# Two-layer streaming encoder step: branch scalars, load order, last tile and five small operations changed at once

## The chip, the cores and the metric

The kernel runs on one core of one Trainium2 chip. The metric is the device time of one execution in microseconds (us). A core has five engines with an instruction queue each, which run side by side and wait for each other by semaphores: PE (TensorE, matmuls; PEld is its weight load), DVE (VectorE), ACT (ScalarE), POOL (GpSimd), and SP, which here only issues DMAs. Each engine takes its instructions strictly in the order in which the program lists them.

## The reference

The reference is one inference step of an encoder with two layers, for a prompt of 512 frames and a sample request of 32 frames with 1024 frames of cache. The 544 frames are carried together, frames along the free dimension (`T` = 544) and 8 tiles of 128 model columns on the partitions. One layer is

```
h = RMSNorm(x);  z = h @ w_in                       (all mixers and gates in one projection)
A = latent attention (q from a rank-256 latent, keys from a rank-128 latent, rotary key)
B = stick-breaking attention (reverse cumulative sums of log(1 - sigmoid))
C = (softmax(Q1 K1) - lambda * softmax(Q2 K2)) V, per-head norm, times (1 - lambda_init)
    lambda = exp(sum(lv0*lv1)) - exp(sum(lv2*lv3)) + lambda_init   (one scalar per layer)
x += w_out(sigmoid(gA)*(A @ wA) + sigmoid(gB)*(B @ wB) + sigmoid(gC)*(C @ wC))
x += w_down(silu(conv3(a)) * u),   [a, u] = RMSNorm(x) @ w_up
```

and besides y the new rows of all caches and the last two rows of the convolution are returned. All matmuls are done in float32r with each operand split in a high and a low part (three products), so each weight tile is first rounded on ACT (high part) and subtracted on DVE (low part).

## The kernel before

**Order of the work.** The program is not written in the order in which it runs. `Sched` (L114) keeps a clock for each engine and a list of fibers, Python generators with a time `ready`. `Sched.run` steps the fiber with the smallest `ready` first; each helper (`act`, `tt`, `ptt`, `dscale`, `mm`, ...) emits one instruction and adds an estimated price to its engine's clock. So the estimated times decide in which order instructions stand in each engine's queue, and after that the queues are fixed. A fiber that is spawned with `low=True` is put behind PE's clock by `LOW` (L138). Constants at L95 to L106 set this planner: `WIDTH` is how many attention fibers may be open at once, `LO` is the place in the list of branch projections from which the last eight attention outputs are loaded back.

**Weights.** `Stream.loader` (L214) is a fiber that issues one DMA on SP for each weight tile (128x1024 f32, 512 KB), in the order of `plan()`, into 4 buffers `ws`. `Stream.splitter` (L228) splits each tile in halves of 512 columns into 4 buffers `wx`: high part on ACT (L340), low part on DVE (L347).

**Start of the program** (`run`, L2143). SP issues the gains of layer 0 (L2162), then the four vectors of lambda (L2186), the first weight tile, and the eight input tiles `x_in` (L2250). Each input tile is scaled and split on ACT and DVE (`norm_tile`, L528); its squares are summed over the tiles, and `norm_rows` (L555) makes the reciprocal root: a split of the sum, four matmuls with a constant matrix, logarithm and exponential on ACT.

**Per layer.** The loop at L2178 loads ACT's table, loads the vectors of lambda into a `tf` buffer and works out lambda and four gain columns by some ten tiny operations on DVE and one exponential on ACT (L2189 to L2204); these are emitted at once, outside of the planner, and for both layers into the same small tiles. Then `attention` runs: projections of the units (`qkv_tasks`, 48 matmuls of 128x272 for each tile of 128 columns), gate projections between them (`gate_tasks`, 24 a layer, 48 matmuls each), and the chains of the three mixers: units 0 to 3 stick-breaking (`sb`), 4 to 7 differential (`df`), 8 to 11 latent (`ml`). `GATES` (L42) tells how many gate projections follow the projections of each of the 12 units, the last digit being those that run with low priority beside the last unit. Then follow the branch projections `br_tasks`, `out_tasks`, the up projections (a Strassen form for most), and the down projections `down_tasks` (L2115) in two halves of 11 tiles each.

**Two-operand operations on GpSimd.** `ptt` (L350) emits a tensor_tensor on POOL. It is used in five places: the low part of the differential keys (`to_stack`, L662), the running sums of the stick-breaking sample (L943, seven of 128x64 a unit) and prompt (`sb_sum`, L1098), and the rotary product of the latent queries (L1521, 64x544). POOL also rounds high parts (`pscale`, L367), scales softmax rows, and issues some DMAs.

**End.** The last eight down projections add into x by halves of 272 columns on DVE; `fin` (L2238) stores the whole tile as y (layer 1) or as xs (layer 0). With `both=True` a `gemm` (L445) does the two halves of a tile side by side in two PSUM banks; with `both=False` all steps of the first half come before those of the second. After the planner has run dry, the convolution rows are stored (L2248).

Of the kernel before, what the change touches and what calls it, by code (L numbers as in the profile page):

```python
# [17 lines left out]
L = 2  # L18
# [23 lines left out]
GATES = "403111221315"  # L42
# [58 lines left out]
WIDTH = 12  # L101
LOW = 100.0
LO = 2
# [96 lines left out]
class Stream:  # L200
# [5 lines left out]
    def __init__(self, K, ap, pool):  # L206
        self.K, self.nc, self.s, self.ap, self.pool = K, K.nc, K.s, ap, pool
        self.plan = plan()
        self.early = [key for key, _ in self.plan[:2]]
        self.raw, self.parts = {}, {}  # L210
        self.s.spawn(self.loader(), daemon=True)
        self.s.spawn(self.splitter(), daemon=True)

    def loader(self):  # L214
        s, o = self.s, 0
        for key, n in self.plan:
# [94 lines left out]
class Kern:  # L311
# [216 lines left out]
    def norm_tile(self, m, x, gcol, l, R, late=0, tag="h"):  # L528
# [23 lines left out]
        if m == 7:  # L552
            self.s.spawn(self.norm_rows(R), daemon=True)
# [99 lines left out]
    def to_stack(self, dst, name, z, scale=1.0):  # L653
# [248 lines left out]
    def sb_sample(self, d, U):  # L902
# [38 lines left out]
        for kt in range(6, -1, -1):  # L941
            o, n = col(kt), col(kt + 1)
            self.ptt(R[:, o:o + 64], R[:, n:n + 64], t[:, n:n + 64], ALU.add)  # L943
# [150 lines left out]
    def sb_sum(self, U, h, j, t, sp):  # L1094

        if j < 3:
            yield from self.s.need(U, ("t", h, j + 1))
            self.ptt(t[:, 128:], t[:, 128:], U["t", h, j + 1][0], ALU.add)  # L1098
# [400 lines left out]
    def ml_prep(self, l, u, M, d):  # L1499

        def q_task(h):
# [13 lines left out]
            def post(box):  # L1515
# [5 lines left out]
                self.ptt(z[r], z[r], M["tq"][0][r], ALU.mult)  # L1521
# [593 lines left out]
    def down_tasks(self, l, hf, acts, X, fin):  # L2115
        def mk(m):
# [10 lines left out]
            def post(box):  # L2127
                x = X[m][0]
                for h in range(2):
                    g, c = yield from self.half(box, h)  # L2130
                    self.tt(x[:, c], g, x[:, c], ALU.add)
                    self.unbank(box, h)
                    yield
                if hf == 1:
# [4 lines left out]
                                     chunk, lambda k: self.s.need(acts, 11 * hf + k), free, True)  # L2139
# [3 lines left out]
    def run(self):  # L2143
        tc, nc, a, s = self.tc, self.nc, self.a, self.s
        with tc.tile_pool(name="P", bufs=1) as P, tc.tile_pool(name="ps", bufs=1, space=PSUM) as ps, \
# [5 lines left out]
            self.eps = P.tile([128, 1], F32, tag="eps", name="eps")  # L2151
            nc.vector.memset(self.eps, EPS)
            self.lamv = P.tile([128, 1], F32, tag="lamv", name="lamv")
            self.nlam = P.tile([128, 1], F32, tag="nlam", name="nlam")
            lw = P.tile([128, 8], F32, tag="lw", name="lw")
# [6 lines left out]
            nc.sync.dma_start(out=self.gpl[0], in_=a["gains"][0])  # L2162
            R = {}

# [13 lines left out]
            for l in range(L):  # L2178
                nc.scalar.preload_act_table_set("natural_log_exp_and_others")
                self.gp = self.gpl[l]  # L2180
                if l == 0:
                    s.spawn(consts(), 9000.0)
                    self.ws = Stream(self, a["wts"], P)
                lam_init = 0.8 - 0.6 * math.exp(-0.3 * l)
                lv = self.t(P, [128, T], "tf")
                nc.sync.dma_start(out=lv[:, :256], in_=a["lam"][l])  # L2186
                l4 = lv[:, :256].rearrange("p (a b c) -> p a b c", a=2, b=2)
                l2 = lv[:, 256:384].rearrange("p (a c) -> p a c", a=2)
                nc.vector.tensor_tensor(out=l2, in0=l4[:, :, 0], in1=l4[:, :, 1], op=ALU.mult)  # L2189
                nc.vector.tensor_reduce(out=lw[:, 0:2], in_=l2, op=ALU.add, axis=AX.X)  # L2190
                nc.scalar.activation(out=lw[:, 2:4], in_=lw[:, 0:2], func=AF.Exp)
                nc.vector.tensor_tensor(out=lw[:, 4:5], in0=lw[:, 3:4], in1=lw[:, 2:3], op=ALU.subtract)
                nc.vector.tensor_scalar(out=self.nlam, in0=lw[:, 4:5], scalar1=-lam_init, scalar2=None, op0=ALU.add)
                nc.vector.memset(self.lamv[:32], 1.0)
                nc.vector.tensor_copy(out=self.lamv[32:64], in_=self.nlam[32:64])
                sg = self.gain(G_SUB)
                nc.vector.tensor_scalar(out=sg, in0=sg, scalar1=1.0 - lam_init, scalar2=None, op0=ALU.mult)
                dq = self.gain(G_DQ)
                nc.vector.tensor_scalar(out=dq, in0=dq, scalar1=0.125, scalar2=None, op0=ALU.mult)
                mq = self.gain(G_QE, 2)  # L2200
# [309 lines left out]
```

## Time and profile before

| what | us |
|---|---|
| median of 3 runs (2080.33 to 2081.0) | 2080.8 |
| the profiled execution, its own time | 2081.47 |
| its span in the profile, first to last instruction | 2079.6 |
| PE busy | 2024.5 (97%) |
| DVE busy | 1619.2 (78%) |
| ACT busy | 1308.3 (63%) |
| POOL busy | 501.9 (24%) |
| mean granted TensorE clock | 0.997 |

The span is what the views of the trace cover; the execution's own time is 1.87 us longer. A busy share is an average over stages: layer 0 lies in about 0 to 1044 us of the span, layer 1 behind it, and in each the attention takes the first half. In a row of the timeline the first number is the start, the second the time, `xN` how many instructions were merged, and the bracket how long the engine sat idle before and what ended that. PEclk is the granted clock as a part of the full 2.4 GHz; 0.50 is 1.2 GHz.

### The profile page before, as it was taken

How to read it: one execution, taken by the hardware profiler on the slowest of the kernel's cores; microseconds unless marked ns; L12 is line 12 of the kernel's file. 1: busy time of each engine (PE TensorE's matmuls, PEld its weight loads, DVE VectorE, ACT ScalarE, POOL GpSimd, SP SyncE). 2: the span in 40 equal slices, each digit the busy share in tenths (PEclk: the TensorE clock that was granted, in tenths of full speed). 3: DMA queues.
4: the chain of work that ended last, by engine and by line, in shares of the span. 5: the costliest groups of instructions: out<-in, count | busy, mean ns of one | idle time of the engine just before them, and what ended most of it. 6: DMA issues, size and time to landing. Idle time of an engine off the chain costs nothing.

```text
span 2079.6 us, 41484 instructions
## 1 busy us (share of the span) xinstructions
PE 2024.5 (97%) x15638; PEld 1974.1 (95%) x15638; DVE 1619.2 (78%) x3435; ACT 1308.3 (63%) x2905; POOL 501.9 (24%) x810
## 2 busy tenths in 40 slices
PE   7999999999999999999989999999899999999999
PEld 7999999888999999999989999998899999999999
DVE  7888888888685996598567878988886869955973
ACT  6887676877554564366368777668775545644651
POOL 1333332334200221032023443313341002210310
PEclk9999999999999999999999999999999999999999
DMA  6333342321663222332433334343216622223332
GB/s 205 104 104 124 120 157 93 129 73 48 212 199 107 80 95 83 110 102 82 133 119 98 109 124 132 122 133 102 83 39 223 203 93 92 94 80 102 102 90 87
DMA packets 86216, 238.42 MB, mean 115 GB/s; under 512 B 10304, under 2 KB 11200, under 8 KB 86016
## 3 DMA queue, kind: packets, MB, share of 16 engines
q1 hardware_dynamic: 82240, 223.51, 33.7%
q0 software_dynamic: 3776, 12.26, 1.7%
q8 instruction: 123, 2.02, 0.4%
q14 instruction: 77, 0.63, 0.1%
HBM read 201.52 MB, written 34.21 MB: 113 GB/s over the span
## 4 chain that ended last, share of the span: by engine, by line
PE 75%; DVE 14%; ACT 5%; issue 4%; POOL 1%; DMA 1%; SPq 0%; POOLq 0%; ACTq 0%; DVEq 0%
PE z L410 40%; PE g L410 25%; PE pv L410 8%; DVE wx L347 2%; PE z L416 2%; DVE tf L347 1%; ACT p L340 1%; DVE w L347 1%; ACT wx L340 1%; ACT w L340 1%; DVE tr L347 1%; DVE kk L347 1%; ACT tf L340 1%; DVE nm L372 1%; DVE sgl L355 1%
## 5 line engine op out<-in xcount | busy, mean ns | idle before, releaser
L410 PE MATMUL g<-h,wx 128*128 128x272 f32 x5208 | 757.2, 292 | 9.1 <-ACT wx L340 9.0
L410 PEld LDWEIGHTS g<-h,wx 128*128 128x128 f32 x5208 | 695.6, 189 | 17.5 <-ACT wx L340 9.0
L410 PE MATMUL z<-act,wx 128*128 128x272 f32 x4632 | 586.7, 288 | 5.6 <-DVE wx L347 5.6
L410 PEld LDWEIGHTS z<-act,wx 128*128 128x128 f32 x4632 | 581.5, 189 | 6.7 <-DVE wx L347 6.7
L340 ACT ACTIVATE wx<-ws 128x512 fp32r<-128x512 f32 (+2 forms) x554 | 307.0, 555 | 383.9 <-PE z L410 257.1
L347 DVE TENSOR_TENSOR wx<-ws,wx 128x512 fp32r<-128x512 f32 (+2 forms) x554 | 343.7, 621 | 208.7 <-ACT wx L340 205.2
L410 PE MATMUL z<-h,wx 128*128 128x272 f32 x1368 | 179.6, 290 | 0.0
L410 PEld LDWEIGHTS z<-h,wx 128*128 128x128 f32 x1368 | 175.5, 191 | 0.0
L340 ACT ACTIVATE w<-z 128x512 fp32r<-128x512 f32 (+9 forms) x212 | 90.9, 440 | 52.4 <-PE pv L410 27.7
L347 DVE TENSOR_TENSOR tf<-g,rstd 128x272 f32<-128x272 f32 x184 | 79.8, 434 | 31.9 <-PE g L410 25.8
L2061 POOL COPY conv<-ap 128x2 f32<-128x2 f32 x34 | 20.7, 610 | 316.9 <-DVE ap L347 316.9
L1924 POOL COPY conv<-ap 128x2 f32<-128x2 f32 x10 | 19.5, 1953 | 299.8 <-DVE ap L347 299.8
L410 PE MATMUL pv<-w,vst 128*128 128x512 f32 (+3 forms) x352 | 85.5, 325 | 4.9 <-DVE w L347 4.3
L2048 POOL COPY ap<-gp 128x2 f32<-128x2 f32 x34 | 63.5, 1866 | 81.9 <-ACT wx L340 60.0
L340 ACT ACTIVATE wy<-ws 128x512 fp32r<-128x512 f32 x68 | 42.9, 630 | 60.1 <-PE z L410 34.9
L368 POOL TENSOR_SCALAR tr<-tf 128x544 fp32r<-128x544 f32 (+2 forms) x66 | 49.1, 744 | 128.2 <-ACT tf L340 89.2
L355 DVE SCALAR_TENSOR_TENSOR cc<-ap,gp,cc 128x546 f32<-128x546 f32 x88 | 69.2, 786 | 4.0 <-ACT cc L340 3.8
L340 ACT ACTIVATE p<-p 128x512 f32<-128x512 f32 (+4 forms) x160 | 70.6, 465 | 0.9
L340 ACT ACTIVATE wx<-sgl 128x512 fp32r<-128x512 f32 x102 | 63.4, 627 | 11.1 <-PE z L410 7.1
L347 DVE TENSOR_TENSOR wx<-sgl,wx 128x512 fp32r<-128x512 f32 x102 | 67.8, 686 | 2.3 <-ACT wx L340 2.2
L368 POOL TENSOR_SCALAR kk<-kk 64x1024 fp32r<-64x1024 f32 x32 | 40.7, 1272 | 118.3 <-DVE kk L347 101.0
L347 DVE TENSOR_TENSOR w<-z,w 128x512 fp32r<-128x512 f32 (+5 forms) x124 | 55.8, 465 | 15.3 <-ACT w L340 14.6
(274 smaller groups left out, 3673.0 us busy)
## 6 DMA issues: line engine op xcount, KB each, us to landing
ws<-wts SPq DMA_DIRECT2D x246, 512.0 KB, 3.6
ws<-wts SPq DMA_DIRECT2D x56, 256.0 KB, 3.0
ws<-wts SPq DMA_DIRECT2D x36, 384.0 KB, 3.0
sgl<-sig SPq DMA_DIRECT2D x46, 272.0 KB, 3.2
ws<-wts SPq DMA_DIRECT2D x32, 320.0 KB, 3.0
sig<-tf SPq DMA_DIRECT2D x36, 272.0 KB, 2.1
tf<-od POOLq DMA_DIRECT2D x24, 272.0 KB, 4.7
od<-oa SPq DMA_DIRECT2D x16, 272.0 KB, 2.3
```

Source lines behind the costliest of these rows:

```text
L340: self.nc.scalar.activation(out=out, in_=in_, func=func, **kw)
L347: self.nc.vector.tensor_tensor(out=out, in0=in0, in1=in1, op=op)
L355: self.nc.vector.scalar_tensor_tensor(out=out, in0=in0, scalar=scalar, in1=in1, op0=op0, op1=op1)
L368: self.nc.gpsimd.tensor_scalar(out=out, in0=in_, scalar1=s1, scalar2=1.0, op0=ALU.mult, op1=ALU.mult)
L372: self.nc.vector.tensor_reduce(out=out, in_=in_, op=op, axis=AX.X, negate=negate)
L410: self.nc.tensor.matmul(out=out, lhsT=lhsT, rhs=rhs, start=start, stop=stop, skip_group_check=not chk)
L416: self.nc.tensor.transpose(out, in_, self.ident[:p, :p])
L1924: nc.gpsimd.tensor_copy(out=cv[:, 0:2], in_=ap[:, 546:548])
L2048: nc.gpsimd.tensor_copy(out=ap[:, 0:2], in_=self.gain(G_ST + 2 * i, 2))
L2061: nc.gpsimd.tensor_copy(out=cv[:, 0:2], in_=ap[:, 546:548])
```

## The change

- The scalars of both layers (lambda and the scaled gains) are made by a fiber `lams`, spawned at the planner's 40 us in layer 0, into columns of one tile; nothing of this is left in the loop over the layers. The exponential and the small DVE operations go through the planner's helpers.
- The first weight tile is loaded in two halves by DMAs issued on ACT's queue, as are the gains of layer 0; the loader starts with the second tile, at the planner's 0.1 us, so that SP issues the eight input tiles first. The planner's estimates of when the input tiles land are changed (4.7 us + 0.8 us a tile in place of 3.0 + 1.1).
- `norm_rows` of the first norm of a layer is spawned 1 us later in the planner's time.
- All five `ptt` become `tt`, on DVE.
- `GATES`: one gate projection goes from behind unit 7 to behind unit 4. `WIDTH` 12 to 11, `LOW` 100 to 50, `LO` 2 to 3.
- In the last layer y is stored by halves as each is added, and the last of the eight tiles is done with `both=False`. The convolution rows are stored before the last down projection, in both layers.

```diff
-GATES = "403111221315"
+GATES = "403121211315"
-WIDTH = 12
-LOW = 100.0
-LO = 2
+WIDTH = 11
+LOW = 50.0
+LO = 3
@@ class Stream, __init__
+        s, t = K.s, K.t(pool, [128, 1024], "ws")
+        s.tok["ws"].pop()
+        for c in (0, 512):
+            self.nc.scalar.dma_start(out=t[:, c:c + 512],
+                                     in_=ap[:128 * 1024].rearrange("(p c) -> p c", p=128)[:, c:c + 512])
+        self.raw[self.plan[0][0]] = (t, 4500.0)
+        self.s.spawn(self.loader(), 100.0, daemon=True)
@@ loader
-        for key, n in self.plan:
+        for key, n in self.plan[1:]:
@@ norm_tile
-            self.s.spawn(self.norm_rows(R), daemon=True)
+            self.s.spawn(self.norm_rows(R), self.s.cur.ready + (1000.0 if tag == "h" else 0.0), daemon=True)
@@ to_stack; the same in sb_sample, sb_sum and ml_prep
-                self.ptt(out, x, f(hi), ALU.subtract)
+                self.tt(out, x, f(hi), ALU.subtract)
@@ down_tasks
+                    if y is not None:
+                        self.store(y[m][:, c], x[:, c])
-                                     chunk, lambda k: self.s.need(acts, 11 * hf + k), free, True)
+                                     chunk, lambda k: self.s.need(acts, 11 * hf + k), free, y is None or m < 7)
@@ run
-            nc.sync.dma_start(out=self.gpl[0], in_=a["gains"][0])
+            nc.scalar.dma_start(out=self.gpl[0], in_=a["gains"][0])
+            self.ws = Stream(self, a["wts"], P)
+            def lams():
+                for l in range(L):
+                    lv = yield from self.tf()
+                    nc.sync.dma_start(out=lv[:, :256], in_=a["lam"][l])
+                    s.cur.ready += 5000.0
+                    yield
...
+                    self.tt(l2, l4[:, :, 0], l4[:, :, 1], ALU.mult)
+                    yield
+                    nlam, lamv = lw[:, 1 + l:2 + l], lw[:, 3 + l:4 + l]
+                    self.red(lw[:, 8:10], l2, ALU.add)
+                    s.give("tf")
+                    yield
+                    self.act(lw[:, 10:12], lw[:, 8:10], AF.Exp)
+                    yield
...
             for l in range(L):
                 nc.scalar.preload_act_table_set("natural_log_exp_and_others")
                 self.gp = self.gpl[l]
+                self.nlam, self.lamv = lw[:, 1 + l:2 + l], lw[:, 3 + l:4 + l]
                 if l == 0:
                     s.spawn(consts(), 9000.0)
-                    self.ws = Stream(self, a["wts"], P)
-                lv = self.t(P, [128, T], "tf")
-                nc.sync.dma_start(out=lv[:, :256], in_=a["lam"][l])
...
-                nc.scalar.activation(out=lw[:, 2:4], in_=lw[:, 0:2], func=AF.Exp)
...
+                    s.spawn(lams(), 40000.0)
@@ end of the layer
-                    lst += self.down_tasks(l, 1, acts, X, fin)
+                    dn = self.down_tasks(l, 1, acts, X, fin, a["y"] if l == L - 1 else None)
+                    lst += dn[:-1] + [convs, dn[-1]]
...
-                    self.store(a["convo"][l], self.conv)
@@ x_in
-        self.s.cur.ready += 3000.0 + 1100.0 * m
+        self.s.cur.ready += 4700.0 + 800.0 * m
```

## Rows read from the trace of the kernel before

**Rows 1.** The page: busy time of the engines, and the chain by engine.
```profile
PE 2024.5 (97%) x15638; PEld 1974.1 (95%) x15638; DVE 1619.2 (78%) x3435; ACT 1308.3 (63%) x2905; POOL 501.9 (24%) x810
...
PE 75%; DVE 14%; ACT 5%; issue 4%; POOL 1%; DMA 1%; SPq 0%; POOLq 0%; ACTq 0%; DVEq 0%
```

**Rows 2.** Windows: length, busy us by engine (instructions), PEclk, DMA share, GB/s.
```profile
0.00:20.00 20.00, 10.92 (x63) 10.60 (x64) 12.58 (x28) 12.73 (x21) 0.66 (x6) 1.00 0.88 297
...
40.00:360.00 320.00, 315.39 (x2369) 301.42 (x2369) 269.44 (x634) 239.78 (x579) 112.13 (x210) 1.00 0.36 119
360.00:520.00 160.00, 150.34 (x1127) 141.44 (x1126) 133.70 (x289) 122.14 (x307) 59.87 (x80) 1.00 0.26 84
...
1080.00:1400.00 320.00, 317.20 (x2381) 303.38 (x2380) 265.33 (x631) 235.98 (x571) 113.31 (x207) 1.00 0.36 117
1400.00:1560.00 160.00, 149.46 (x1106) 140.31 (x1104) 131.86 (x288) 119.08 (x306) 60.29 (x81) 0.99 0.24 78
```

**Rows 3.** Timeline of the first 20 us.
```profile
1.26 0.42 SPq L2186 DMA_DIRECT2D tf<-lam  x1
...
2.19 1.85 SPq L2253 DMA_DIRECT2D tf<-x  x4
...
6.98 1.41 ACT L340 ACTIVATE h<-tf,gp 128x544 fp32r<-128x544 f32 x2 [2.46 <-DMA tf<-x]
...
8.29 0.61 ACT L340 ACTIVATE wx<-ws 128x512 fp32r<-128x512 f32 x1
...
8.96 9.45 PE L410 MATMUL g<-h,wx 128*128 128x272 f32 x48 [8.96 <-ACT wx L340]
...
18.24 6.89 PE L410 MATMUL z<-h,wx 128*128 128x272 f32 x54
```

**Rows 4.** Timeline of the boundary between the layers.
```profile
1044.13 0.38 SPq L2186 DMA_DIRECT2D tf<-lam  x1
...
1047.37 0.29 DVE L2189 TENSOR_TENSOR tf<-tf 128x128 f32<-128x128 f32 x1 [3.28 <-DMA tf<-lam]
...
1049.34 0.39 PE L410 MATMUL pv<-tr,cr 128*128 128x272 f32 x1 [2.95 <-ACT tr L340]
...
1050.85 1.05 PE L410 MATMUL pv<-tr,cr 128*128 128x272 f32 x3 [1.12 <-DVE tr L347]
...
1051.70 9.10 PE L410 MATMUL z<-h,wx 128*128 128x272 f32 x54
```

**Rows 5.** Window of 2 us behind the boundary's gap, same columns as rows 2.
```profile
1052.00:1054.00 2.00, 2.00 (x11) 2.00 (x11) 0.79 (x2) 1.08 (x2) 0.00 (x0) 0.50 0.75 242
```

**Rows 6.** Timeline of the last DMA issues.
```profile
2076.49 0.33 SPq L442 DMA_DIRECT2D y<-x  x1
2076.91 0.38 SPq L442 DMA_DIRECT2D convo<-conv  x1
```

**Rows 7.** Window over the whole span, instructions of L351 alone.
```profile
0.00:2079.60 2079.60, 100.34 (x128) 1.00 0.36 115
```

**Rows 8.** Groups of DVE by form: 0 to 30, 40 to 520, 1400 to 1560 us.
```profile
L347 DVE TENSOR_TENSOR wx<-ws,wx 128x512 fp32r<-128x512 f32 x7 | 4.8, 687 | 3.8 <-ACT wx L340 3.8
...
L347 DVE TENSOR_TENSOR an<-z,an 128x64 f32<-128x64 f32 x4 | 0.8, 210 | 0.0
...
L347 DVE TENSOR_TENSOR wx<-ws,wx 128x512 fp32r<-128x512 f32 x19 | 17.4, 917 | 1.8 <-ACT wx L340 1.7
```

**Rows 9.** Timeline of POOL in the latent stage of layer 0.
```profile
393.12 1.32 POOL L351 TENSOR_TENSOR wk<-wk,tq 64x544 f32<-64x544 f32 x1 [0.77 <-DVE wk L355]
394.42 0.61 POOL L368 TENSOR_SCALAR tr<-tf 128x512 fp32r<-128x512 f32 x1
```

**Rows 10.** Timeline of PE in the latent stages of both layers.
```profile
395.96 0.62 PE L410 MATMUL z<-tr,cr 128*128 128x256 f32 x3 [2.76 <-DVE tr L347]
...
1428.13 0.62 PE L410 MATMUL z<-tr,cr 128*128 128x256 f32 x3 [1.17 <-DVE tr L347]
```

**Rows 11.** Waits of PE, 1400 to 1560 us: total, times, longest.
```profile
PE z L416 <- POOL p L368: 2.8, 4, 1.4
```

More of the change, by code (lines that the diff above doesn't have):

```diff
@@ L2113, in strassen, with down_tasks @@
         return go
-    def down_tasks(self, l, hf, acts, X, fin):
+    def down_tasks(self, l, hf, acts, X, fin, y=None):
         def mk(m):
@@ L2150, in run @@
             self.cr = P.tile([128, C_W], F32R, tag="cr", name="cr")
[L2151 removed]
+            lw = P.tile([128, 16], F32, tag="lw", name="lw")
+            self.eps = lw[:, 0:1]
             nc.vector.memset(self.eps, EPS)
[L2153 to L2155 removed]
             self.conv = P.tile([128, 4 * NI], F32, tag="conv", name="conv")
@@ L2180, in run @@
                 self.gp = self.gpl[l]
+                self.nlam, self.lamv = lw[:, 1 + l:2 + l], lw[:, 3 + l:4 + l]
                 if l == 0:
                     s.spawn(consts(), 9000.0)
-                    self.ws = Stream(self, a["wts"], P)
-                lam_init = 0.8 - 0.6 * math.exp(-0.3 * l)
-                lv = self.t(P, [128, T], "tf")
-                nc.sync.dma_start(out=lv[:, :256], in_=a["lam"][l])
[L2187 to L2190, printed above, removed]
-                nc.scalar.activation(out=lw[:, 2:4], in_=lw[:, 0:2], func=AF.Exp)
[L2192 to L2200, printed above, removed]
-                nc.vector.tensor_scalar(out=mq, in0=mq, scalar1=MLA_SCALE, scalar2=None, op0=ALU.mult)
-                for h in range(2):
-                    r = slice(64 * h, 64 * h + 64)
-                    nc.vector.tensor_tensor(out=mq[r, h:h + 1], in0=mq[r, h:h + 1], in1=self.gain(G_KN)[r], op=ALU.mult)
+                    s.spawn(lams(), 40000.0)
                 self.gtag = "g"
@@ L2238, in fin @@
                     def fin(m, x):
-                        self.store(a["y"][m] if l == L - 1 else xs[m], x)
                         if l < L - 1:
+                            self.store(xs[m], x)
                             yield from self.norm_tile(m, x, G_MIX, l + 1, R)
@@ L2243, in fin, with convs @@
                             yield
-                    lst += self.down_tasks(l, 1, acts, X, fin)
+                    def convs():
+                        self.store(a["convo"][l], self.conv)
+                        yield
+                    dn = self.down_tasks(l, 1, acts, X, fin, a["y"] if l == L - 1 else None)
+                    lst += dn[:-1] + [convs, dn[-1]]
                     s.spawn(self.tasks(lst), s.free["pe"])
                     s.run()
-                    self.store(a["convo"][l], self.conv)
     def x_in(self, m, R):
```

25 lines of the change are left out of this document (20 added, 5 removed).

## The prediction

> **What bounds the kernel now.** I read the page first: PE is busy for 97% of the span, and the chain that ended last runs on PE for 75% of it and on DVE for 14% [rows 1]. So work moved between other engines is worth only what it does to PE's gaps and to its clock. Second the windows, to see where the gaps are [rows 2]: PE lacks 20.00 - 10.92 = 9.1 us in the first 20 us; in the attention of layer 0 it lacks 4.6 us (40 to 360) and 9.7 us (360 to 520, the latent units), in that of layer 1 2.8 and 10.5 us; together 27.6 us for attention. DVE is busy for 84% of these windows (269.44 of 320, 133.70 of 160). Third the timeline where a gap is long: the start, the boundary of the layers, the end [rows 3, 4, 6]. Last POOL's own rows and PE's waits, for the operations that change engine [rows 7 to 11].
>
> **The change part by part.**
>
> *Boundary.* The reader sees in rows 4 that SP issues the lambda vectors at 1044.13, that DVE sits for 3.28 us until they land, and that PE, out of matmuls, waits 2.95 us for the split of the sum of squares on ACT, which stands in ACT's queue behind the exponential of lambda; then 1.12 us more for the low part on DVE. After that gap PE goes at a granted 0.50, 1.2 GHz [rows 5]: 54 matmuls take 9.10 us, where 54 took 6.89 us at the start [rows 3, 4]. In the new kernel lambda and gains of both layers are ready long before, and nothing of them stands in a queue here. The norm's split can follow the last square and the table load, and the norm's matmuls come 1 us later in the planned order, behind some eight more matmuls of the projection (1 us by 127.6 ns, which is 6.89/54). Gain 2.95 + 1.12 + (9.10 - 6.89) = 6.3 us. At least 2.95 us (the wait for lambda alone), at most 7, since the three norm matmuls in 1.05 us were slow too. What is late next here is the split behind ACT's table load; the projections of the next tiles hide it. Storing the convolution rows earlier takes one issue off SP there and costs nothing beside 8 us of matmuls; without that cover, 0.4 us.
>
> *Where lambda goes.* Some ten tiny operations a layer, twice, enter DVE's and ACT's queues near 40 us. If the vectors landed late, DVE would sit as it did at the boundary, 3.28 us; behind it would queue weight splits and PSUM evacuations, and PE would wait for those. They are planned 5 us behind their DMA, where 1044.13 to 1047.37 was 3.2, and PE has a list of projections there: I take nothing, bounds 0 and +3.3.
>
> *Start.* Before the input tiles SP issued gains, lambda and a weight tile: lambda and weights took 2.19 - 1.26 = 0.93 us, the gains some 0.42 more (as lambda's issue), so the first tile is issued 1.35 us earlier. It was 4.79 us from its issue (2.19) to its use (6.98); lambda's at the boundary took 3.24 with nothing ahead. I take 3.8, a gain of 1.0, nearer to the small end, because the weight halves still move beside it. ACT did two input tiles before the first weight half (6.98, 8.29); now the weights are planned first, half of 1.31, 0.65 us. Sum 3.0 us off the first matmul's 8.96. The first 48 matmuls then took 9.45 us against 6.1 at 127.6 ns, and I leave that stretch as long as it is. The second weight tile is moved past eight inputs on SP, but its first use comes after 48 matmuls. Bounds: 0.4 us if bytes set the pace (the 128 KB of lambda by 297 GB/s; the DMA engines are at 0.88 in these 20 us [rows 2]), 3.6 if the tile lands in 3.24.
>
> A rule of the pages speaks against this part. The Trainium skill, "DMA: Bandwidth & Descriptors", section "Issuing engines are not separate DMA queues", says that DMAs from several engines share the same 16 DMA engines and that a second issuer saves only issue time. By it the start would gain the 1.35 us of issue and the time would be 2080.8 - (1.35 + 6.3 + 0.4 + 1.8) = 2071.0, near the first rival below; the row with 0.88 bears it out in part.
>
> *Two-operand operations.* POOL spends 100.34 us on 128 of them [rows 7]: by the code 56 of 128x64, 16 of 64x512, 16 of 64x544, 16 of 128x256, 16 of 128x128, 8 of 128x32. On DVE 128x512 takes 687 ns with POOL quiet and 128x64 takes 210 [rows 8], so 1.065 ns a column and 142 ns a call: 56 x 0.210 + 16 x 0.687 + 16 x 0.721 + 16 x 0.415 + 16 x 0.278 + 8 x 0.176 = 47.0 us more on DVE. Over the four attention windows DVE goes from 800 to 847 of 960 us, 88%. PE's idle there is 27.6 us by 800 us of DVE work, 3.4%; at that rate the 47 us cost 1.6 us. On the other side, POOL's queue is in PE's gaps: at 393.12 a rotary product of 1.32 us stood ahead of the rounding that PE then waited for, 2.76 us [rows 9, 10]; layer 1 has the same stop with 1.17, and four stops of 2.8 us behind softmax rows scaled on POOL [rows 10, 11]. That is 6.7 us in which a shorter queue helps; I take half, 3.4. Net gain 1.8 us. Bounds: a loss of 23.5 us, if half of the 47 shows up on PE, and a gain of 10.1, half of the idle of the latent stages.
>
> The same DVE split of 128x512 takes 687 ns at the start and 917 in the latent stage of layer 1, where POOL is busy for 60 of 160 us [rows 2, 8]. The Trainium skill, "SBUF — State Buffer", section "Who interferes with whom", says that a DVE instruction with two SBUF inputs contends with a GpSimd one that reads SBUF, and that the loser waits for the whole instruction. By that rule the moved operations, all with two SBUF inputs, become exposed to what stays on POOL, 47.0 x 917/687 = 63 us as an estimate, and the 16 us more would at 3.4% take 0.5 us off the gain: 2069.8.
>
> *Order.* `GATES`, `WIDTH`, `LOW`, `LO` change no work. One gate projection, 48 x 127.6 ns = 6.1 us, leaves the place just ahead of the latent units, where PE idles most, for one in the middle of the differential units. Both layers, ordered by different planner states, differ by 1.8 and 0.8 us of idle in like stages, so I take nothing, bounds 6.1 us either way in a layer.
>
> *End.* The convolution issue (2076.91) falls away behind the last y (2076.49), and the last store is half as large: 0.4 us, bounds 0 and 0.8. Until then the half-by-half order of the last tile hides the first half's addition and store beside 33 matmuls.
>
> **The sum.** 3.0 + 6.3 + 1.8 + 0.4 = 11.5 us. The profiled execution took 2081.47 us, 1.87 more than its span and 0.67 above the median; 2081.47 - 11.5 = 2070.0, and by the median 2080.8 - 11.5 = 2069.3.
>
> **Rivals.** Parts other than attention give 9.7 us.
> - Bytes pace the start: the gain there is 0.4, the time 2071.9. For it the DMA share of 0.88; against it that the weight half and the first tile are all that the first matmul needs.
> - The boundary keeps its gap, because the norm's own chain (table load, split, low part) still ends after PE has run dry: only 2.95 is won, 2080.8 - (3.0 + 2.95 + 0.4 + 1.8) = 2072.7. For it the 1.12 us wait, which is not lambda's; against it the 1 us of matmuls put ahead.
> - The filler is missed: the projection taken from ahead of the latent units leaves 6.1 us of idle in one of the layers, none of which is used elsewhere, and the POOL gain with it: 2080.8 - 9.7 + 6.1 = 2077.2, no change that can be told. For it, these stages hold 20.2 of the 27.6 us of idle.
> - The latent stages close up: with short queues on POOL, half of their 20.2 us goes: 2080.8 - 9.7 - 10.1 = 2061.0. For it rows 9 to 11; against it that most of PE's waits there are for DVE and ACT, which get no shorter.
> - The other side: DVE becomes the bound of attention. It sits at 84% as a mean, and each weight split and PSUM evacuation queues behind the added operations; half of the 47 us reaches PE, 2080.8 - 9.7 + 23.5 = 2094.6. It decides from 13.9 us, 30% of the added work. Against it, PE idles only 4.6 and 2.8 us in the long windows with DVE at 84%.
>
> **How the numbers follow.** 0.2% or 4.2 us is about what a measurement of this kernel can tell from no change. Chances: the forecast 0.45 (its own range 2064 to 2075), bytes 0.10, kept gap 0.10, missed filler 0.11, closed latent stages 0.17, DVE bound 0.07. Faster by over 0.2%: 0.45 + 0.10 + 0.10 + 0.17 = 0.82; within 0.11; slower 0.07. The range 2059 to 2077 leaves out the DVE case, most of the missed filler and the far end of the closed stages.
>
> **What would show it.** Right: the first matmul near 6.0; no PE gap over 1 us and a granted clock of 1.00 from the last down projection of layer 0 into the second tile of layer 1; POOL near 400 us busy and DVE near 1666; the last y half as the last DMA. Wrong: PE's idle over 30 us in the attention windows, DVE waits of PE longer than 1 us in the stick-breaking units, or a boundary where PE still waits for ACT's split and drops to 0.50.

## The result and the profile after

The kernel after takes 2056.1 us (median of 4 runs, 2055.59 to 2059.91) against 2080.9 beside it (2080.33 to 2082.02); the ratio is 0.9881, 95% interval 0.987 to 0.9893. That is 24.8 us faster where 11.5 were forecast, and below the range given. The profiled execution, 2059.91, is the slowest of the four; its span is 2057.8, so the traces account for 21.8 us. The line numbers of helpers are 6 higher in the kernel after (L347 is L353 there, L410 is L416, L351 is not used).

The page of the kernel after, engines and chain, beside [rows 1]:

```profile
PE 2018.6 (98%) x15638; PEld 1974.9 (96%) x15638; DVE 1636.0 (80%) x3563; ACT 1312.9 (64%) x2905; POOL 411.9 (20%) x682
...
PE 78%; DVE 12%; ACT 5%; issue 2%; DMA 2%; POOL 1%; ACTq 0%; SPq 0%; DVEq 0%; POOLq 0%
```

The weight loads are busy as long as before (1974.1 and 1974.9), so all that the span lost (21.8) is time in which no weight was loaded: 105.5 us before, 82.9 now. PE's busy time fell by 5.9 although the same 15638 matmuls ran, so part of what stood there as work was something else; 2.2 of it is the slow clock behind the boundary's gap (9.10 to 6.93 us, below). The Trainium skill, "Trainium Kernel Development and Optimization", section "Performance Expectations", calls matmul busy time a bad metric for how close a kernel is to its bound, and the busy share of LDWEIGHTS a good one. The trace agrees: for the same work the weight loads' time moved by 0.8 us, the matmuls' by 5.9.

Windows of the kernel after, columns as in [rows 2]; layer 1 moved 14 us ahead, so its windows are too:

```profile
0.00:20.00 20.00, 11.43 (x55) 10.69 (x56) 10.47 (x16) 12.49 (x20) 0.66 (x6) 0.91 0.81 292
40.00:360.00 320.00, 317.29 (x2404) 306.00 (x2403) 279.83 (x713) 240.87 (x582) 84.55 (x154) 1.00 0.38 122
360.00:520.00 160.00, 153.03 (x1150) 144.28 (x1149) 138.51 (x313) 127.00 (x321) 48.21 (x75) 1.00 0.25 79
1066.00:1386.00 320.00, 318.43 (x2416) 307.05 (x2416) 276.94 (x690) 238.03 (x571) 78.15 (x150) 1.00 0.36 118
1386.00:1546.00 160.00, 154.94 (x1143) 146.35 (x1142) 136.78 (x309) 125.09 (x314) 49.68 (x79) 0.98 0.25 80
```

DVE is busier (279.83 where 269.44 was), PE and its weight loads too. With marks in PE's timeline (first matmul of the second unit, of the latent stage, of the branch projections, of the next layer) each span splits into stages, in us:

| stage | before | after |
|---|---|---|
| start, to the second unit | 32.4 | 31.7 |
| stick-breaking and differential units, layer 0 / 1 | 346.1 / 345.8 | 342.2 / 341.2 |
| latent units, layer 0 / 1 | 164.9 / 167.5 | 161.5 / 162.6 |
| branch to down projections, layer 0 / 1 | 496.5 / 496.6 | 497.8 / 498.1 |
| boundary | 26.2 | 19.0 |
| behind the last matmul | 3.6 | 3.6 |

By the unrounded marks attention gives 16.7 us, the boundary 7.2, the start 0.7; the projections lose 2.8 (a stop of 1.01 us for DVE at 551.52, absent before, and its like in layer 1).

The timeline of the boundary after, for [rows 4]:

```profile
1036.52 1.28 ACT L2218 ACT_TABLE_LOAD   x1
1038.35 0.64 ACT L346 ACTIVATE tr<-rstd 128x544 fp32r<-128x544 f32 x1
...
1039.17 1.65 PE L416 MATMUL z<-h,wx 128*128 128x272 f32 x12
...
1040.66 0.66 PE L416 MATMUL pv<-tr,cr 128*128 128x272 f32 x4
...
1041.15 6.93 PE L416 MATMUL z<-h,wx 128*128 128x272 f32 x54
```

PE has matmuls on both sides of the norm's four, without a bracket, and the 54 matmuls that took 9.10 us take 6.93; the granted clock in 1042 to 1044 is 1.00 where [rows 5] had 0.50.

The start after, for [rows 3]:

```profile
0.82 1.81 SPq L2276 DMA_DIRECT2D tf<-x  x4
...
5.57 0.63 ACT L346 ACTIVATE wx<-ws 128x512 fp32r<-128x512 f32 x1 [2.07 <-DMA ws<-wts]
...
6.89 0.59 PE L416 MATMUL g<-h,wx 128*128 128x272 f32 x1 [6.89 <-ACT h L346]
...
12.54 0.63 ACT L346 ACTIVATE wx<-ws 128x512 fp32r<-128x512 f32 x1 [2.72 <-DMA ws<-wts]
...
13.86 0.39 PE L416 MATMUL g<-h,wx 128*128 128x272 f32 x1 [1.03 <-ACT h L346]
...
19.19 2.05 PE L416 MATMUL z<-h,wx 128*128 128x272 f32 x15
```

The first matmul is 2.07 us earlier, yet the second projection starts at 19.19 where it was 18.24: at 12.54 ACT stands 2.72 us for the second weight tile, which SP now issues behind eight inputs, and input tiles 4 and 5 queue behind it. This execution also lost its clock there: the window 0 to 20 above shows a granted 0.91, and 16 to 18 alone 0.50. Ten other profiled kernels of the experiments have the same load order and lambda out of the loop; their clock is 1.00 in these 20 us, their second projection starts at 17.8 to 18.7, and their second unit at 30.3 to 31.2, where it is 31.7 here and was 32.4 before. So the new start gains 1.2 to 2.1 us where the clock holds, and 0.7 in this execution.

The latent stages after, PE's stops where [rows 10] had 2.76 and 1.17 us:

```profile
395.05 0.62 PE L416 MATMUL z<-tr,cr 128*128 128x256 f32 x3 [0.49 <-DVE tr L353]
...
1415.83 0.63 PE L416 MATMUL z<-tr,cr 128*128 128x256 f32 x3 [0.67 <-DVE tr L353]
```

The waits of PE for `p` on POOL [rows 11] are gone from the window 1386 to 1546. Now the moved operations, in groups by form over the whole span: POOL before, then DVE before, then DVE after.

```profile
L351 POOL TENSOR_TENSOR wk<-wk,tq 64x544 f32<-64x544 f32 x16 | 25.1, 1567 | 22.0 <-DVE wk L355 21.9
L351 POOL TENSOR_TENSOR w<-w,p 128x64 f32<-128x64 f32 x56 | 23.3, 417 | 16.6 <-DVE p L355 12.6
L351 POOL TENSOR_TENSOR u<-tf,u 64x512 fp32r<-64x512 f32 x16 | 22.6, 1414 | 13.8 <-ACT u L340 12.9
```

```profile
L347 DVE TENSOR_TENSOR pk<-ws,pk 128x512 fp32r<-128x512 f32 x68 | 52.8, 795 | 3.0 <-ACT pk L340 2.8
L347 DVE TENSOR_TENSOR u<-wk,u 128x544 fp32r<-128x544 f32 x16 | 14.4, 901 | 2.2 <-ACT u L340 2.2
```

```profile
L353 DVE TENSOR_TENSOR pk<-ws,pk 128x512 fp32r<-128x512 f32 x68 | 47.3, 715 | 0.3
L353 DVE TENSOR_TENSOR w<-w,p 128x64 f32<-128x64 f32 x56 | 13.5, 241 | 2.2 <-POOL w L945 0.5
L353 DVE TENSOR_TENSOR u<-wk,u 128x544 fp32r<-128x544 f32 x16 | 11.8, 737 | 0.1
L353 DVE TENSOR_TENSOR wk<-wk,tq 64x544 f32<-64x544 f32 x16 | 11.8, 737 | 0.3
...
L353 DVE TENSOR_TENSOR u<-tf,u 64x512 fp32r<-64x512 f32 x16 | 11.0, 686 | 0.5
```

Each moved operation costs DVE about what was forecast (737 ns for 721, 686 for 687, 241 for 210), about half of what it took on POOL (1567, 1414, 417). All 128 take 49.1 us on DVE. Yet DVE's busy time rose by 16.8 us, not by 47: its other operations got shorter (`pk` 795 to 715 ns, `u` 901 to 737).

Waits of the weight loads in attention, 32 to 535 us: total, times, longest; before, then after.

```profile
PEld pv L410 <- DVE w L347: 6.2, 9, 1.1
PEld z L410 <- DVE tr L347: 4.1, 4, 3.0
PEld z L416 <- POOL p L368: 2.1, 4, 0.8
```

```profile
PEld z L416 <- DVE tr L353: 2.7, 6, 0.7
PEld pv L416 <- DVE w L353: 2.2, 4, 1.1
...
PEld z L422 <- POOL p L374: 0.3, 2, 0.2
```

Summed over all rows of this view, the weight loads waited 16.4 us for DVE and 2.8 for POOL, now 8.9 and 0.3. PE waits less for the engine that got more work. For the longest of these waits, 2.97 us at 395.96, the reason is in the rows: while POOL made the rotary product of 1.32 us at 393.12 [rows 9], two casts on DVE took 1.53 us, 1.35 of it the second; a weight split and `tr` stood behind them in DVE's queue. The same two casts, before, then after:

```profile
392.95 1.53 DVE L359 CAST b<-kk 64x32 fp32r<-64x32 f32 x2
```

```profile
393.50 0.78 DVE L365 CAST b<-kk 64x32 fp32r<-64x32 f32 x2
```

Beside 11 of the 16 rotary products of the kernel before a DVE instruction takes 1.2 to 1.9 us, of forms that take 0.2 to 0.8 elsewhere. That the other waits came from this too is not shown.

The last DMA issue, for [rows 6], is half of y; the convolution rows were issued at 2039.49. The span ends 3.6 us behind the last matmul, as before.

```profile
2054.75 0.33 SPq L448 DMA_DIRECT2D y<-x  x1
```

### The profile page after: what moved, and what is told of

Read it like the earlier page. It is cut to its first block, busy times and chain, and to the rows that moved or that the text cites. A ratio compares the mean times of both kernels' runs of the same rounds, so it can differ in the third digit from the quotient of the medians.

```text
span 2057.8 us, 41462 instructions
## 1 busy us (share of the span) xinstructions
PE 2018.6 (98%) x15638; PEld 1974.9 (96%) x15638; DVE 1636.0 (80%) x3563; ACT 1312.9 (64%) x2905; POOL 411.9 (20%) x682
## 4 chain that ended last, share of the span: by engine, by line
PE 78%; DVE 12%; ACT 5%; issue 2%; DMA 2%; POOL 1%; ACTq 0%; SPq 0%; DVEq 0%; POOLq 0%
PE z L416 40%; PE g L416 28%; PE pv L416 8%; PE z L422 2%; DMA ws<-wts 2%; DVE wx L353 2%; ACT p L346 1%; DVE tf L353 1%; DVE w L353 1%; ACT w L346 1%; ACT tf L346 1%; DVE pk L353 1%; ACT wx L346 1%; DVE b L353 1%; DVE p L361 1%
## 5 line engine op out<-in xcount | busy, mean ns | idle before, releaser
L416 PE MATMUL g<-h,wx 128*128 128x272 f32 x5208 | 760.2, 292 | 10.8 <-ACT h L346 7.9
L416 PEld LDWEIGHTS g<-h,wx 128*128 128x128 f32 x5208 | 697.9, 190 | 21.0 <-ACT h L346 8.1
L416 PE MATMUL z<-act,wx 128*128 128x272 f32 x4632 | 588.0, 288 | 4.3 <-DVE wx L353 4.3
L416 PEld LDWEIGHTS z<-act,wx 128*128 128x128 f32 x4632 | 583.1, 189 | 5.2 <-DVE wx L353 5.2
L353 DVE TENSOR_TENSOR wx<-ws,wx 128x512 fp32r<-128x512 f32 (+2 forms) x554 | 339.4, 613 | 203.9 <-ACT wx L346 200.8
L416 PE MATMUL z<-h,wx 128*128 128x272 f32 x1368 | 178.0, 287 | 2.1 <-DVE x L353 2.1
L416 PEld LDWEIGHTS z<-h,wx 128*128 128x128 f32 x1368 | 173.4, 188 | 2.5 <-DVE x L353 2.5
L346 ACT ACTIVATE w<-z 128x256 f32<-128x256 f32 (+9 forms) x212 | 91.2, 440 | 42.4 <-PE pv L416 21.4
L353 DVE TENSOR_TENSOR tf<-g,rstd 128x272 f32<-128x272 f32 x184 | 79.9, 434 | 25.5 <-PE g L416 19.0
L416 PE MATMUL pv<-w,vst 128*128 128x512 f32 (+3 forms) x352 | 81.6, 322 | 1.6 <-DVE w L353 1.6
L353 DVE TENSOR_TENSOR wx<-sgl,wx 128x512 fp32r<-128x512 f32 x102 | 67.7, 685 | 2.3 <-ACT wx L346 2.2
L353 DVE TENSOR_TENSOR w<-z,w 128x512 fp32r<-128x512 f32 (+5 forms) x124 | 55.7, 464 | 11.7 <-ACT w L346 10.8
```

What stands on the lines that cost most here:

```text
L346: self.nc.scalar.activation(out=out, in_=in_, func=func, **kw)
L353: self.nc.vector.tensor_tensor(out=out, in0=in0, in1=in1, op=op)
L416: self.nc.tensor.matmul(out=out, lhsT=lhsT, rhs=rhs, start=start, stop=stop, skip_group_check=not chk)
```

## The experiments

Theory: the operations on DVE and the new order constants are worth something only together. Rivals: any change of the order deals the waits anew, by chance; or one part carries the gain. Ratios are to the kernel before on the same chip. Where an edit is long, its fence tells it in words.

**One part alone.** Kernel before and the five operations on DVE:

```
-    self.ptt(...)
+    self.tt(...)          # all five
```

> Before, with the five two-operand operations of GpSimd on VectorE and nothing else. The changed kernel gained 24.7 us where 11.5 were forecast; by the two profiles the attention of the two layers gained about 7 and 9 us, and not 1.8. Theory queue (the gain is POOL's queue, shorter chains): 10 to 16 us faster, 2065 to 2071. Theory order (the planner's constants did it): 0 to 3 us faster. Theory reshuffle (any change of the planner's prices moves the attention by several us either way, no part owns the gain): anywhere from 5 us slower to 8 faster, and the four parts will not add up.

2081.68 us, 0.9999 (0.9989 to 1.0009): nothing. The four constants alone:

```
-GATES = "403111221315"; WIDTH = 12; LOW = 100.0; LO = 2
+GATES = "403121211315"; WIDTH = 11; LOW = 50.0;  LO = 3
```

> Before, with GATES, WIDTH, LOW and LO of the change and nothing else; no instruction is added or removed. Theory queue: within 3 us of before. Theory order: 8 to 14 us faster, 2067 to 2073, all of it in the attention windows. Theory reshuffle: 5 us slower to 8 faster.

2096.76, 1.007 (1.0057 to 1.0082): a loss of 14. The scalars alone:

```
+    s.spawn(lams(), 40000.0)      # nothing of lambda left in the loop
+    self.s.spawn(self.norm_rows(R), ... + 1000.0 ...)
```

> Before, with the branch scalars of both layers made once by a fiber at the planner's 40 us, and norm_rows 1 us later in the planned order; the rest as before. All theories of the boundary: 6 to 7 us faster, PE without a gap over 1 us there and a granted clock of 1.00; if the norm's own chain kept the gap, 3 us. Theory reshuffle adds up to 5 us either way, in the attention windows.

2080.42, 0.9995 (0.9986 to 1.0005). The boundary is 19.0 us as in the kernel after, 7.2 won, but the first layer's attention takes 519.3 where it took 511.0, with a new stop of 2.63 us for ACT at 154.08. The new start alone:

```
+    (in words) ACT's queue: gains, first weight tile in two halves; SP: inputs first
```

> Before, with the new load order at the start (gains and first weight tile on ACT's queue, input tiles first on SP, the planner's landing times) and nothing else. Forecast of the start: 3 us faster. In the profile of the changed kernel the first matmul starts 2.1 us earlier but the second weight projection 0.95 us later (19.19 after 18.24), because ACT waits 2.7 us for the second weight tile ahead of input tiles that have landed: by that 0 to 1 us faster.

2081.81, 0.9999 (0.999 to 1.0008): nothing. By medians, beside 2082.34, the four sum to a loss of 11 us; the whole change, which has only the new end beside them, wins 25.

**A shift of the order by itself.** `LAT`, the planner's estimate of a hand-over, 125 to 126, in the kernel after and in the one before:

```
-LAT = 125.0
+LAT = 126.0
```

> The changed kernel with the planner's LAT 126 in place of 125: no instruction is added or removed, no part of the change is undone, only near ties in the planned order fall otherwise. Theory reshuffle (the attention's time is a draw of the planned order, and the changed kernel holds a good one): several us slower than the changed kernel, 2060 to 2068, with the loss in the two attention stretches and the boundary unchanged at 19 us. Theories queue and order (a part of the change owns the gain): within 3 us of it, 2053 to 2059.

2055.74, 0.9877 (0.986 to 0.9893).

> The kernel before with the planner's LAT 126 in place of 125, nothing else. Theory reshuffle: the attention stretches (511 and 513 us) move by 3 to 10 us each, either way. Theories queue and order: within 3 us of before.

2084.39, 1.0015 (1.0006 to 1.0024). The attention of the two layers moves by 4.4 and 0.6 us. So this shift moves the kernel before by 3 us and the kernel after not at all. It is one draw for each kernel and doesn't rule chance out; the run of the pair below is the stronger test.

**One part taken back from the kernel after.** All five operations on POOL:

```
-    self.tt(...)
+    self.ptt(...)         # all five
```

> The changed kernel with the two-operand operations back on GpSimd, all else as changed. The operations alone gave nothing (0.9999) and the planner's constants alone cost 14 us. Theory joint (operations and constants only work together, since the constants were right for the shorter POOL queue): 15 to 25 us slower than the changed kernel. Theory queue as first put: 10 us slower. Theory reshuffle: 3 to 15 us slower, and no more than the changed kernel with LAT 126 loses, within 5 us.

2091.11, 1.0043 (1.0028 to 1.0058): 35 us lost, more than any of the theories had. The four constants of before:

```
-GATES = "403121211315"; WIDTH = 11; LOW = 50.0;  LO = 3
+GATES = "403111221315"; WIDTH = 12; LOW = 100.0; LO = 2
```

> The changed kernel with GATES, WIDTH, LOW and LO of before. Theory joint: 10 us or more slower than the changed kernel, about 2066 to 2074 (boundary 7 us and little else gained). Theory reshuffle: 3 to 15 us slower, like the one with LAT 126. Theory queue as first put: within 3 us of the changed kernel.

2071.09, 0.995 (0.9935 to 0.9964), inside the joint theory's range. That it is near the forecast of 2069.3 is luck: its attention gains 7.9 us, where 1.8 were forecast. So in the kernel after the operations are worth 35 us and the constants 15; in the kernel before the operations alone were worth nothing and the constants alone lost 14. The rotary product alone on POOL:

```
-    self.tt(z[r], z[r], M["tq"][0][r], ALU.mult)
+    self.ptt(z[r], z[r], M["tq"][0][r], ALU.mult)
```

> The changed kernel with only the rotary product of the latent queries (64x544, 8 a layer) back on GpSimd. With all five back the kernel took 2091.1 and its latent stages 171.8 and 174.3 us in place of 161.5 and 162.6; the other four operations do not occur in those stages. Theory rotary (in the latent stage, with the new planner constants, the rotary product on POOL is what PE waits for): the latent stages go back to 170 to 175 us, the stick-breaking and differential stages stay at 342, 2074 to 2082 in all. Theory pool (POOL's load as a whole): at most a third of the 35 us, under 2068.

2071.76, 0.9955 (0.9939 to 0.997). It costs the latent stages 5.2 and 5.0 us (166.7 and 167.7 for 161.5 and 162.6) and the stick-breaking and differential stages nothing (342.0, 341.3). The time lies between the two theories and bears out neither. The other four on POOL:

```
-    self.tt(...)
+    self.ptt(...)         # to_stack, sb_sample, sb_sum
```

> Kernel after with four of the five two-operand operations back on GpSimd (running sums, low part of the differential keys); only the rotary product of the latent queries stays on VectorE. All five back cost 35 us (2091), the rotary product alone 16 (2072). If the two groups add: 2056 + 19 = 2075, the loss mostly in the stick-breaking and differential stage (2 to 5 us a layer). If the rotary product is all that counts: 2056 to 2060.

2085.92, 1.0018 (1.0008 to 1.0028). This is outside both forecasts. The stick-breaking and differential stages take 345.9 and 346.8, 3.7 and 5.5 more, to a tenth what all five cost there; but the latent stage of layer 1, in which none of the four occurs, takes 179.8, 17 more. Alone the two groups cost 16 and 30 us, together 35: they do not add. `GATES` alone as before:

```
-GATES = "403121211315"
+GATES = "403111221315"
```

> The changed kernel with GATES of before (the projection back behind unit 7). Undoing all four constants cost 15 us, 2 to 3 us in each stick-breaking and differential stage and 2 to 3 in each latent one. Theory gates: 6 us or more slower, and the stage between units 4 and 7 longer. Else within 3 us.

2081.2, 0.9988 (0.9975 to 1.0002): by medians the place of one gate projection is worth 25 us here (22 by the ratios), in a kernel whose work is the same. The executions spread from 2073.25 to 2085.26; the profiled one, 2075.67, shows 16 of it. `WIDTH` alone as before:

```
-WIDTH = 11
+WIDTH = 12
```

> The changed kernel with WIDTH 12 in place of 11. Theory width (one open fiber less keeps the latent chains from overtaking the projections): 6 us or more slower, in the latent stages. Else within 3 us.

2067.2, 0.9933 (0.9917 to 0.995): 11 us slower, 4.6 and 2.3 of it in the latent stages, as the theory of the width has it. `LOW` alone as before:

```
-LOW = 50.0
+LOW = 100.0
```

> The changed kernel with LOW 100 in place of 50. The low-priority gate projections run only beside the last latent unit, so a change can show only in the last 40 us of each latent stage: within 3 us of the changed kernel by all theories but the one that LOW owns the gain (then 6 us or more slower).

2064.17, 0.9917 (0.9903 to 0.9932), 8 us slower where 3 were expected, with attention as in the kernel after (504.3, 503.6) and 5.1 us more in layer 0's projections. The three constants cost 25, 11 and 8 us one by one, all four only 15: they do not add either. `LO` alone was not run. The old start:

```
-    (in words) ACT's queue: gains, first weight tile in two halves; SP: inputs first
+    (in words) SP: gains, first weight tile, inputs
```

> Kernel after with the old start (first weight tile and gains on SP ahead of the inputs, old landing times for the planner). By the trace the new start gains 0.7 us, so 2057, with attention stages within 1 us of those of the kernel after. By the prediction's term of 3.0: 2059. If a shift of the planner's clock at the start deals the waits of attention anew: 2060 to 2070, with the loss in attention.

2070.52, 0.9948 (0.9933 to 0.9963). At the start itself nothing is lost: these rows of its timeline, with lambda gone from SP, have the second projection at 16.88, 2.3 us ahead of the kernel after and 0.9 to 1.8 ahead of the ten kernels whose clock held (17.72 with the same start in the last run below); its second unit begins at 30.4, as theirs do:

```profile
8.65 8.38 PE L410 MATMUL g<-h,wx 128*128 128x272 f32 x48 [8.65 <-ACT wx L340]
...
16.88 4.30 PE L410 MATMUL z<-h,wx 128*128 128x272 f32 x33
```

The loss is in layer 0's latent stage (173.8 for 161.5); layer 1 takes 501.3. So luck of the deal is not gone from the kernel after: a changed start costs 12 us in a stage that it doesn't touch.

**The pair.** Kernel before with the five operations on DVE and the four constants, nothing else:

```
+    self.tt(...)          # all five
+GATES = "403121211315"; WIDTH = 11; LOW = 50.0;  LO = 3
```

> Kernel before with two parts of the change only: the two-operand operations on VectorE and the four constants of the order (GATES, WIDTH, LOW, LO). Start, boundary and end as before. Joint theory (the two parts are worth nothing or a loss alone and some 17 us together): attention shortened as in the kernel after, by 7 to 10 us a layer, 2081 - 17 = 2064, range 2060 to 2069. Rival (the pair needs the other parts too, because any change of the order deals the waits anew): 2073 to 2090. By the prediction's own terms (1.8 for the operations, nothing for the order): 2079.

2063.55, 0.9913 (0.9899 to 0.9928): the joint theory's number, within 0.5 us. With it the square is complete in one kernel: the operations gain 33 us with the new constants and nothing with the old, the constants gain 18 with the operations on DVE and lose 14 with them on POOL. The time without a weight load in the two attentions makes the square too, in us: before 75.1, operations alone 67.6, constants alone 84.5, both 57.3 (kernel after 57.4). The operations alone do shorten the waits by 7.5; 6.0 of it came back as longer weight loads; behind two stops, 404 to 412 and 1434 to 1446 us both show a granted 0.57 as a mean, stretches at 1.2 GHz among them.

**A version that might be better.** The planner told that the second weight tile lands 3.5 us later:

```
-                s.cur.ready += 5000.0
+                s.cur.ready += 8500.0
```

> A version that may beat both: kernel after, with the planner told that the second weight tile lands 3.5 us later, so that ACT scales input tiles 4 and 5 ahead of its split. In the kernel after ACT stands 2.72 us at 12.54 for that tile and PE 1.03 + 0.43 us behind it. If the stop goes: second projection earlier by 1 to 1.5 us, 2054.7. If order in later stages moves with it: 2052 to 2062, within 0.3% of the kernel after.

2056.58, 0.9877 (0.986 to 0.9893). The time is that of the kernel after: no better version came of it. The edit did not take the stop away. ACT still waits for the second weight tile ahead of input tiles 4 and 5 (2.67 us at 11.77), and PE still stops 0.82 and 0.43 us behind it. The second unit begins 1.4 us earlier (30.3) than in the profile of the kernel after, but so it does in the run with `LAT` 126 (30.4), without this edit: the clock of the first 20 us is 1.00 in both, 0.91 in the kernel after.

**Why the place of a gate counts.** The end of the latent stage of layer 0 in the run with the old `GATES`:

```profile
530.96 0.54 POOL L448 DMA_DIRECT2D od<-oa  x1 [8.60 <-DVE oa L353]
...
531.63 2.31 POOL L860 DMA_DIRECT2D tf<-od  x4
533.93 0.54 POOL L448 DMA_DIRECT2D sig<-tf  x1
...
540.01 0.44 DVE L353 TENSOR_TENSOR tf<-g,rstd 128x272 f32<-128x272 f32 x1 [4.61 <-DMA sig<-tf]
...
541.68 0.42 PE L416 MATMUL z<-w,uv 128*128 128x64 f32 x1 [3.03 <-ACT w L346]
543.78 1.27 PE L416 MATMUL z<-w,uv 128*128 128x64 f32 x5 [1.68 <-DVE w L353]
```

A gate's store (`sig`) stands on POOL behind an output store and four loads. DVE's next evacuation needs its buffer and waits 4.61 us; the last unit's rows queue behind it on DVE, the gate projections that fill PE run out, PE stops twice and goes on at 0.50. The same end in the kernel after: the stores were issued earlier, the evacuation waits only for PE, and 15 gate matmuls are left behind the unit's last:

```profile
521.02 1.06 POOL L448 DMA_DIRECT2D sig<-tf  x1 [6.19 <-DVE w L353]
...
528.44 0.55 POOL L448 DMA_DIRECT2D sig<-tf  x1 [2.38 <-DVE tf L353]
...
532.54 0.44 DVE L353 TENSOR_TENSOR tf<-g,rstd 128x272 f32<-128x272 f32 x1 [0.52 <-PE z L416]
...
533.44 2.12 PE L416 MATMUL g<-h,wx 128*128 128x272 f32 x15
```

The test moves only these stores to SP; PE, DVE and ACT keep their order:

```
-SWG = 18
+SWG = 24
```

> Kernel after with GATES of before, and the stores of the last six gate projections of a layer (sig) issued on SP instead of POOL (SWG 18 to 24); the instructions of PE, DVE and ACT and their order are those of the run with GATES of before alone (2081). In its trace, at the end of the latent stage, od<-oa and four loads tf<-od stand in POOL's queue ahead of a store sig<-tf, which lands at 540.0; the DVE evacuation that needs its buffer waits 4.6 us (4.5 in layer 1), the last unit's rows wait behind it on DVE, PE stops 3.0 + 1.7 us and then runs at 1.2 GHz for 3.4 us worth. Theory (POOL's queue holds the gates' stores): the wait goes, some 4 to 6 us a layer, time 2070 to 2074. Rival (the landing itself is slow, or SP holds the store as long behind a weight load that waits for a buffer): 2079 to 2085, with the wait for sig<-tf still over 3 us.

2075.36, 0.9965 (0.9954 to 0.9976), 5.8 less than with the stores on POOL, where 7 to 11 were expected; the two intervals just touch, and the two traces' attention differs by 6.0. These rows of layer 0:

```profile
527.95 0.42 SPq L448 DMA_DIRECT2D sig<-tf  x1
...
532.25 0.44 DVE L353 TENSOR_TENSOR tf<-g,rstd 128x272 f32<-128x272 f32 x1 [0.92 <-PE g L416]
...
534.09 0.66 ACT L346 ACTIVATE h<-tf 128x544 fp32r<-128x544 f32 x1 [3.07 <-DMA tf<-od]
...
537.48 0.30 PE L416 MATMUL z<-w,uv 128*128 128x64 f32 x1 [2.48 <-ACT w L346]
```

DVE's wait is gone, and PE's stops fall from 4.71 to 3.06 us. Two things changed for this store. On POOL it was issued 2.5 us after its tile was ready and landed 6.0 us after the issue; on SP it was issued at once and landed after 4.2. Which of the two counts more is not shown, so the rival of a slow landing is not ruled out as a part. What is late next is ACT, which stands 3.07 us for an output loaded back, ahead of the unit's `w`. In layer 1 DVE still waits 3.7 us for a store, and the stage gains 1.0. The same in the run with the old start:

> Kernel after with the old start, and the same stores on SP; order of PE, DVE and ACT as in the run with the old start (2070.5), whose layer 0 lost 12 us in the latent stage, with a 5.3 us wait of DVE for a store sig<-tf, a PE stop of 3.0 us behind it, and another part of the loss earlier in the stage. Theory: layer 0 gains 4 to 6 us of it, 2064.5 to 2066.5, layer 1 (no such wait) stays at 501. Rival as in the other run: 2069 to 2073.

2067.28, 0.9932 (0.9917 to 0.9946): 3.2 less, with intervals that overlap; in the traces layer 0's attention takes 513.7 for 518.4. The place of the stores is a part of the loss, about a third by the traces: 6.0 of 16.5 us in the first pair of runs, 4.7 of 14.7 in the second. Where the rest lies is not shown.

## Why the prediction was wrong

- **The step that failed is "Order", where I took nothing**, and with it the net of 1.8 us for the two-operand operations: each was priced alone, and the pair by itself took attention from 1024.3 to 1003.7 us, 20.6 for the 1.8. I took the spread of idle between the two layers (1.8 and 0.8 us) for the size of what an order can do. The runs show attention of one layer between 501.3 and 526.6 us by order and placement alone; with all operations on DVE and the new `GATES` and `WIDTH`, 12 of 14 layers profiled lie between 501.3 and 504.4 (the other two are layer 0 of the runs with the old start); wherever one of these is as before, all lie at 506.3 or above.
- **The measure.** I bounded attention by PE's idle, 27.6 us, and the latent stages by half of their 20.2. By weight loads the same windows of [rows 2] lack 73.4 us (320 - 301.42, and so on), 35.2 of them in the long windows where I saw only 4.6 and 2.8; half of the gain of attention (3.9 + 4.6 us) came there.
- **Operations.** The price on DVE was right by the piece: 49.1 us measured for 47.0 (its own terms add up to 46.8). But DVE's busy time rose by 16.8 only, so the 1.6 us charged to PE for it rested on work that DVE did not get. On the other side I counted 6.7 us of stops at POOL and took half. The weight loads' waits for DVE fell by 7.5 and those for POOL by 2.5, in layer 0's attention alone: I did not reckon with DVE being held up beside POOL's products, as at 392.95. The Trainium skill, "SBUF — State Buffer", section "Who interferes with whom", has a VectorE instruction with two SBUF inputs contend with a GpSimd one that reads SBUF; I turned that against the change. The trace agrees with the rule the other way round, in the change's favour: with less on POOL `pk` went from 795 to 715 ns.
- **Boundary.** Right in its mechanism: 7.2 us for 6.3 (at most 7 stated), the clock stays at 1.00, and the split behind the table load is hidden.
- **Start.** Mis-sized: 0.7 for 3.0 in the profiled execution, 1.2 to 2.1 where the clock held. The first matmul came 2.07 us earlier, but the second weight tile, which I dismissed because "its first use comes after 48 matmuls", is split on ACT ahead of two input tiles. Lambda leaving SP is the gain: the second unit begins at 30.4, 30.5 and 31.0 in three runs with the old load order and lambda out of the loop, at 32.1 with the new order alone. The new load order itself gains nothing there.
- **End.** 0.4 forecast, nothing seen.
- **Rivals.** The latent stages closed up as in that rival, by 8.3 us of its 10.1, and the other stages as much beside. DVE as the bound does not come true: 87% busy in 40 to 360 us, and a shorter stage. The missed filler came the other way round: in the kernel after, putting the projection back cost 25 us.
- What is not settled: why the operations and the constants need each other, and so where in the chains the 18 us lie. Shorter queues on POOL and a DVE that is held up less came together, and no run parts them. Chance in the order is held down by the seven kernels just counted, not shut out: the old start alone cost 14 us. That the place of a store has a part is seen in two pairs of runs; the early stops of the latent stage under the old `GATES` (1.55 us at 402, 1.13 at 425) were not tried.

## What to carry to other kernels

In a kernel whose order is fixed ahead by estimates, parts that gain nothing alone may gain much together, so test them as a set and by taking one back, and give the forecast the width of the order's own spread. Read slack of a busy TensorE from its weight loads, not from matmul time. Moving an operation can also shorten what it leaves beside: DVE got 49.1 us of new work and was busy for 16.8 us more, so a price by load alone was too high. And compare the start of several profiled runs before one of them is explained: a granted clock of 0.91 in one execution looked like a loss of the load order.

## What the runs showed of the hardware

Taking 90 us from POOL (501.9 to 411.9 us busy) went with shorter DVE operations that were not touched: `pk` 128x512 from 795 to 715 ns, `u` 128x544 from 901 to 737. The moved operations take 49.1 us on DVE, the sum over all its instructions rose by 22.1, so the others lost 27 us. With all five back on POOL in the kernel after, `u` is at 900 again; with the rotary product alone or the other four alone it is at 722 and 724, so it depends on what runs beside it. The clearest single case is the cast of 64x32 that takes 1.35 us beside a rotary product of 1.32 us on POOL, and 0.17 us otherwise.

A stop of PE can be paid twice: behind the 3.03 and 1.68 us of the old `GATES` the granted clock is 0.50, as this window (columns as in [rows 2]) shows.

```profile
544.00:546.00 2.00, 2.00 (x10) 2.00 (x11) 1.16 (x6) 0.00 (x0) 1.30 (x3) 0.50 0.47 32
```

Not every stop is. The kernel before has the same stop of 1.98 us in the down projections of both layers; behind the one the clock falls to 0.64 as a mean of 4 us, behind the other it stays at 1.00:

```profile
697.25 1.02 PE L410 MATMUL z<-act,wx 128*128 128x272 f32 x6 [1.98 <-DVE wx L347]
697.00:701.00 4.00, 3.75 (x20) 3.76 (x21) 4.00 (x10) 2.27 (x4) 1.00 (x1) 0.64 0.44 131
...
1733.21 1.02 PE L410 MATMUL z<-act,wx 128*128 128x272 f32 x6 [1.98 <-DVE wx L347]
1733.00:1737.00 4.00, 3.79 (x30) 3.79 (x31) 4.00 (x10) 2.30 (x4) 1.04 (x1) 1.00 0.44 131
```

Behind the 2.76 us at 395.96 [rows 10] it is 1.00 too, from 396 to 400. So a stop's price in clock is read behind that stop, in that execution.
